# Cached keys in half pages with buffers of their own, cached values in three pages, in a decoder step with two interleaved streams

## The chip, the cores and the metric

The kernel runs on one core of one Trainium2 chip. The metric is device time in microseconds (us) of one execution; the figure for a kernel is the median of its runs. A change of about 0.2% (some 3.6 us) is what a measurement of this kernel can tell from none.

The engines named below: PE multiplies matrices (PEld is its weight load), DVE does elementwise work and reductions, ACT does activations and copies with a scale, POOL does small work and issues gathers, SP issues most plain loads and stores. Each engine takes its instructions in the order in which they stand in its own list, and an instruction that waits holds up all that stand behind it.

## The reference, cut to what matters

One step of a decoder layer for two groups of rows that share the weights: a prompt of 1024 tokens, and 8 sample rows that each attend to 8192 cached tokens. The caches are paged (128 tokens to a page, 64 pages for a sample row, found through a page table).

```python
def fox_sample(q, k, v, logf, k_pool, v_pool, logf_pool, page_table):
    k_all = jnp.concatenate([k_pool[page_table].reshape(B, past, H, hd), ...], axis=1)
    v_all = jnp.concatenate([v_pool[page_table].reshape(B, past, H, hd), ...], axis=1)
    lf_all = jnp.concatenate([logf_pool[page_table].reshape(B, past, H), logf], axis=1)
    c = jnp.cumsum(lf_all, axis=1)
    return fox_attend(q, k_all, v_all, c[:, past:], c, qpos, kpos)     # softmax(q k / 8 + c_q - c_k) v
...
for each group:                                   # prompt, then sample
    x = x + merge_heads(attention, gating, ..., w_o)
    x = x + cross_attend(rmsnorm(x), memory, w_cq, w_co)
    x = x + (silu(gate) * val) @ w_down           # gate, val: causal convolution of rmsnorm(x) @ w_up
y = rmsnorm(x)
```

All numbers are 32-bit floats. The prompt's large products are done as three products of a high and a low part.

## The kernel before, in words

**Two streams.** `prompt()` is a Python generator that writes out the prompt's work stage by stage; `sample()` is another, for the 8 sample rows. The loop at the end of `build` (lines 1923 to 1942) draws from the prompt and, at a rate set by `PACE` for each stage, steps the sample in between. So the text order of the program is an interleaving of both. A scheduler then goes through it with its own model of how long things take, gives out tile buffers as they come free in that model, and fixes the list of each engine. These lists are what the chip runs.

**The sample's first part, `decode()`** (from line 1374). For each sample row `b` there are 16 chunks `ch`; a chunk is 128 x 2048 numbers (1 MB): partition p holds four tokens of half a page. For the keys, `kstep` (line 1425) takes a `KV()` tile, POOL issues an indirect DMA that gathers a chunk (line 1428), DVE multiplies it by the query (lines 1435 and 1444) and sums over each head's 64 elements (1436 and 1448). In stages whose name starts with `att` this is done in four pieces of 512 columns, in some others (`mid`, or while `held`) in two of 1024, otherwise in one of 2048. After 16 chunks there are the softmax steps (`soft_max`, `soft_all`, `soft_exp`). For the values, `vstep` (line 1487) gathers a chunk into a `KV()` tile (1489), and PE multiplies it by the probabilities with four matmuls, one for each quarter of its columns, each on a strip of 32 rows of the accumulator `dv` (1495). Two chunks of values are handled together, 18 chunks after the keys of the same numbers. The gates' cache is gathered by `gates_scan` at chunk 11: an indirect DMA into one `D2()` tile, an ACT copy that swaps tokens and heads (line 1407) into another, and a running sum on DVE (1408).

**The sample's second part, `sample_rest()`** (from line 1611): output projection, cross-attention over 256 memory rows for each sample row, and the gated MLP. Its weights come by POOL's queue in tiles of 1 MB (`page`, line 1568), all in `KV()` tiles. The up-projection works in 11 groups (lines 1761 to 1797): each loads two `KV()` tiles and then issues 64 matmul instructions on `dv` (1774) that alternate between the two tiles, the second one first. ACT copies the result (1786), PE transposes it (1790), ACT copies it back (1791). After the gate (1802 to 1807) the down-projection uses 11 more tiles one after the other (331), and a norm gives the output (1827, 1828).

**Buffers.** `KV()` is one ring of `NKV = 4` tiles of 128 x 2048; `D2()` is a ring of 5 tiles of 128 x 512 that holds queries, gates and many small things of the second part. A tile can be filled again when the last instruction that reads it is done.

**The end of the prompt.** `final` (line 1354) scales the last four tiles of rows by their norm on DVE (1361) and SP stores them (1362). The prompt's large matmuls in its last stage are on lines 272 to 274.

Of the kernel before, what the change touches and what calls it, by code (L numbers as in the profile page):

```python
# [7 lines left out]
F32 = mybir.dt.float32  # L8
# [3 lines left out]
AF = mybir.ActivationFunctionType  # L12
# [37 lines left out]

NKV = 4
VLAG = 2
# [26 lines left out]
def build(nc, tc, ctx, a, phases=None):  # L79
# [42 lines left out]

    def KV():
        return dpool.tile([P, 2048], F32, tag="kv", bufs=NKV, name=nm("kv"))

    def sm(shape, tag, bufs=2, dt=F32):
# [31 lines left out]
    def D2(n=512, dt=F32):  # L158
        return dpool.tile([P, 512], dt, tag="d2", bufs=5, name=nm("d2"))[:, :n]

# [1213 lines left out]
    def decode():  # L1374
# [26 lines left out]

        def gates_scan(b):
            lg = D2()
            nc.gpsimd.indirect_dma_start(lg, None, a["cache_logf"], off(lidx[:, b : b + 1]))
            A = D2()
            Ah = A.rearrange("p (h k) -> p h k", k=64)
            nc.scalar.activation(Ah, lg.rearrange("p (k h) -> p h k", h=8), AF.Copy)
            nc.vector.tensor_tensor_scan(A, rmask, A, 0.0, op0=ALU.mult, op1=ALU.add)
            return A

# [14 lines left out]
        def kstep(b, ch, st):  # L1425
            qb, s = st
            kv = KV()
            nc.gpsimd.indirect_dma_start(kv, None, a["cache_k"], off(kidx[:, b, ch : ch + 1]))  # L1428
            kvv = kv.rearrange("p (k c) -> p k c", c=512)
            if phase[0][:3] == "att":  # L1430

                for i in range(4):
                    yield 0.2
                    with behind(ENG.DVE):
                        nc.vector.tensor_tensor(kvv[:, i, :], kvv[:, i, :], qb, op=ALU.mult)
                        nc.vector.tensor_reduce(
                            s[:, ch * 4 + i, :], kvv[:, i, :].rearrange("p (h d) -> p h d", d=64), axis=AX.X, op=ALU.add
                        )
                return 0.2
            sp = KS if phase[0][:3] == "mid" or held[0] else 1  # L1440
            m = 4 // sp
            with behind(ENG.DVE):
                for i in range(0, 4, m):
                    nc.vector.tensor_tensor(  # L1444
                        kvv[:, i : i + m, :], kvv[:, i : i + m, :], qb.unsqueeze(1).broadcast_to((P, m, 512)), op=ALU.mult
                    )
                for i in range(0, 4, m):
                    nc.vector.tensor_reduce(  # L1448
                        s[:, ch * 4 + i : ch * 4 + i + m, :].rearrange("p k h -> p (k h)"),
                        kvv[:, i : i + m, :].rearrange("p k (h d) -> p (k h) d", d=64),  # L1450
                        axis=AX.X,
                        op=ALU.add,
                    )
            return 1

# [31 lines left out]
        def vstep(b, ch, st, dv, kv):  # L1487
            s = st[1]
            nc.gpsimd.indirect_dma_start(kv, None, a["cache_v"], off(kidx[:, b, ch : ch + 1]))  # L1489
            kvv = kv.rearrange("p (k c) -> p k c", c=512)  # L1490

            def mm(after=None):
                with tc.issue_after(after) if after else behind(ENG.PE):
                    for j in range(4):
                        mmul(  # L1495
                            dv[32 * j : 32 * j + 32, :],
                            s[:, ch * 4 : ch * 4 + 4, :].rearrange("p k h -> p (k h)"),
                            kvv[:, j, :],
                            start=(ch == 1),
                            stop=(ch == 15),  # L1500
                            tile_position=(0, 32 * j),
                        )

            return mm
# [22 lines left out]
        for g in range(8 * 16 + 16 + VLAG + 2):  # L1527
# [8 lines left out]
            if b < 8:  # L1536
                left = yield from kstep(b, ch, st[b])
                if ch == 11:
                    A[b] = gates_scan(b)
                if ch == 13:  # L1540
# [406 lines left out]
_IN = [  # L1947
    "x", "xT", "xs", "xsT", "cache_k", "cache_v", "cache_logf", "cmk", "cmv", "stT", "pt", "mem", "memT",
    "cpack", "gpack", "b_f", "g_sgu_v", "ws00", "bs00", "wsT", "w_in", "w_o", "w_cq", "w_ck", "w_cv", "w_co",
# [8 lines left out]
def layout(np, i):  # L1958
# [15 lines left out]
    for m in range(2):  # L1974
# [13 lines left out]
        "x": f(x), "xT": f(x.T), "xs": f(xs), "xsT": f(xs.T.reshape(8, P, 8).transpose(1, 0, 2)),  # L1988
        "cache_k": f(n["cache_k"]).reshape(-1, 4 * AW), "cache_v": f(n["cache_v"]).reshape(-1, 4 * AW),
        "cache_logf": f(n["cache_logf"]).reshape(-1, 64 * NH),  # L1990
        "cmk": f(n["cache_mem_k"][0]).reshape(NB, NMEM, D), "cmv": f(n["cache_mem_v"][0]).reshape(NB, NMEM, D),
# [43 lines left out]
```

## Time and profile before

| what | value |
|---|---|
| runs, median (lowest to highest) | 1792.71 us (1792.19 to 1794.31) |
| the profiled execution, time | 1793.69 us |
| its span | 1791.7 us |
| PE busy | 1735.9 us, 97% of the span |
| DVE busy | 1399.9 us, 78% |
| ACT busy | 733.5 us, 41% |
| POOL busy | 488.3 us, 27% |
| moved by DMA | 521.06 MB, 291 GB/s on average |
| granted TensorE clock, mean | 0.993 |

How to read it: the shares are averages over stages that differ. The profile of a stretch says which engine was busy throughout; the lists of waits say what ended an engine's idle time; and the timeline of one engine gives the moments at which a buffer came free and the load into it was issued. Line numbers in the profile are those of the kernel before.

### The profile page before, as it was taken

The numbers are of one execution on the slowest core, as the hardware profiler recorded it, in microseconds if no ns is written. First come the engines' busy times: TensorE is split into PE (matmuls) and PEld (weight loads), VectorE is DVE, ScalarE is ACT, GpSimd is POOL, SyncE is SP. The second block draws the span as 40 slices with busy tenths as digits, with TensorE's granted clock in tenths as the row PEclk, the third lists the DMA queues.
The fourth block names the chain that finished last, engine by engine and source line by source line (L and its number), as shares of the span: only waits on it lengthen the run. The fifth ranks groups of instructions, "written<-read, shape, count | busy, mean of one in ns | idle before, by whom it ended". The sixth has DMA issues, their size and how long they took to land.

```text
span 1791.7 us, 25124 instructions
## 1 busy us (share of the span) xinstructions
PE 1735.9 (97%) x9653; PEld 1285.7 (72%) x9653; DVE 1399.9 (78%) x1733; ACT 733.5 (41%) x1374; POOL 488.3 (27%) x461
## 2 busy tenths in 40 slices
PE   8999999889999999999999999999999999999997
PEld 5787777655677666767777777766666778768875
DVE  4689658989788986989999999898885549855344
ACT  6332355566643635333333244335353233333232
POOL 1252234443222332333322223433322112102110
PEclk9999999999999999999999999999999999999999
DMA  8786798777697975779788788988879587568982
GB/s 291 297 304 226 294 334 319 259 264 244 254 403 279 363 299 224 282 285 345 290 301 313 291 317 311 376 306 346 320 280 350 214 306 249 191 260 297 359 310 80
DMA packets 157074, 521.06 MB, mean 291 GB/s; under 512 B 20874, under 2 KB 40842, under 8 KB 124186
## 3 DMA queue, kind: packets, MB, share of 16 engines
q0 software_dynamic: 57168, 341.14, 50.0%
q1 hardware_dynamic: 92874, 165.73, 26.5%
q10 hardware_dynamic: 6912, 12.59, 1.9%
q8 instruction: 76, 1.25, 0.3%
q14 instruction: 44, 0.36, 0.1%
HBM read 495.47 MB, written 23.93 MB: 290 GB/s over the span
## 4 chain that ended last, share of the span: by engine, by line
PE 53%; issue 9%; DMA 8%; DVE 6%; ACT 2%; POOL 2%; POOLq 0%; DVEq 0%; ACTq 0%; SPq 0%
DMA kv<-cache_v,io 6%; PE ba L272 6%; PE ba L274 6%; PE ba L273 6%; PE dv L1495 4%; PE bb L272 3%; PE bb L273 3%; PE bb L274 3%; PE ba L1063 1%; DVE s L1448 1%; PE ba L1064 1%; PE ba L1065 1%; PE dv L331 1%; DMA kv<-cache_k,io 1%; PE dv L1774 1%
## 5 line engine op out<-in xcount | busy, mean ns | idle before, releaser
L235 ACT ACTIVATE wh<-wr 128x1024 fp32r<-128x1024 f32 (+2 forms) x220 | 228.6, 1044 | 443.3 <-PE ba L273 142.3
L236 DVE TENSOR_TENSOR wl<-wr,wh 128x1024 fp32r<-128x1024 f32 (+2 forms) x220 | 262.7, 1200 | 165.1 <-PE ba L274 57.4
L1428 POOL DMA_INDIRECT kv<-cache_k,io x128 | 186.9, 1460 | 606.8 <-DVE s L1448 327.2
L1444 DVE TENSOR_TENSOR kv<-kv,d 128x1024 f32<-128x1024 f32 (+1 forms) x156 | 258.0, 1681 | 32.6 <-DMA kv<-cache_k,io 32.6
L1448 DVE TENSOR_REDUCE s<-kv 128x16 f32<-128x1024 f32 (+1 forms) x156 | 258.4, 1672 | 0.0
L1489 POOL DMA_INDIRECT kv<-cache_v,io x128 | 160.8, 1256 | 239.4 <-PE dv L1495 155.2
L272 PE MATMUL ba<-u,wh 128*128 128x512 f32 x528 | 209.3, 397 | 0.0
L274 PE MATMUL ba<-u,wl 128*128 128x512 f32 x528 | 209.0, 396 | 0.0
L273 PE MATMUL ba<-u,wh 128*128 128x512 f32 x528 | 208.5, 395 | 0.5 <-DVE u L239 0.5
L272 PE MATMUL ba<-wh,u 128*128 128x512 f32 (+1 forms) x495 | 186.1, 379 | 0.9 <-ACT u L235 0.9
L273 PE MATMUL ba<-wl,u 128*128 128x512 f32 (+1 forms) x495 | 185.1, 375 | 1.3 <-DVE wl L236 1.3
L274 PE MATMUL ba<-wh,u 128*128 128x512 f32 (+1 forms) x495 | 183.4, 375 | 0.0
L1495 PE MATMUL dv<-kv,s 128*32 128x512 f32 x1024 | 127.1, 598 | 1.6 <-DMA kv<-cache_v,io 1.6
L274 PEld LDWEIGHTS ba<-u,wl 128*128 128x128 f32 x528 | 99.2, 188 | 29.0 <-issue 6.5
L272 PEld LDWEIGHTS ba<-u,wh 128*128 128x128 f32 x528 | 99.3, 188 | 26.4 <-issue 4.8
L273 PEld LDWEIGHTS ba<-u,wh 128*128 128x128 f32 x528 | 99.2, 188 | 25.2 <-issue 2.3
L272 PEld LDWEIGHTS ba<-wh,u 128*128 128x128 f32 x495 | 93.0, 188 | 25.0 <-issue 6.5
L272 PE MATMUL bb<-u,wh 128*128 128x512 f32 x272 | 108.7, 400 | 0.0
L274 PE MATMUL bb<-u,wl 128*128 128x512 f32 x272 | 108.0, 398 | 0.0
L273 PE MATMUL bb<-u,wh 128*128 128x512 f32 x272 | 107.9, 397 | 0.0
L273 PEld LDWEIGHTS ba<-wl,u 128*128 128x128 f32 x495 | 93.0, 188 | 20.1 <-DVE wl L236 1.9
L274 PEld LDWEIGHTS ba<-wh,u 128*128 128x128 f32 x495 | 92.9, 188 | 19.5 <-issue 1.6
(454 smaller groups left out, 3310.6 us busy)
## 6 DMA issues: line engine op xcount, KB each, us to landing
wr<-w_up SPq DMA_DIRECT2D x88, 512.0 KB
kv<-w_up POOLq DMA_DIRECT2D x22, 1024.0 KB
wr<-w_down SPq DMA_DIRECT2D x40, 512.0 KB
kv<-w_down POOLq DMA_DIRECT2D x11, 1024.0 KB
wr<-w_in SPq DMA_DIRECT2D x16, 512.0 KB
wr<-w_o SPq DMA_DIRECT2D x16, 512.0 KB
wr<-w_cq SPq DMA_DIRECT2D x16, 512.0 KB
wr<-w_co SPq DMA_DIRECT2D x16, 512.0 KB
```

Source lines behind the costliest of these rows:

```text
L235: nc.scalar.activation(h, src, AF.Copy)
L236: nc.vector.tensor_tensor(l, src, h.bitcast(F32), op=ALU.subtract)
L272: mmul(out, sh, mh, start=(i == 0), stop=False)
L273: mmul(out, sh, ml, start=False, stop=False)
L274: mmul(out, sl, mh, start=False, stop=(i == n - 1))
L331: mmul(ps[32 * j : 32 * j + 32, :w], xT[:, k, :] if nk == 8 else xT[:, k * 8 : k * 8 + 32], raw[:, q, j * w : (j + 1) * w], start=(k == 0) ...
L1063: mmul(pss[i], mh[k][:, tb], wh, start=(k == korder[0]), stop=False)
L1428: nc.gpsimd.indirect_dma_start(kv, None, a["cache_k"], off(kidx[:, b, ch : ch + 1]))
L1444: nc.vector.tensor_tensor(kvv[:, i : i + m, :], kvv[:, i : i + m, :], qb.unsqueeze(1).broadcast_to((P, m, 512)), op=ALU.mult)
L1448: nc.vector.tensor_reduce(s[:, ch * 4 + i : ch * 4 + i + m, :].rearrange("p k h -> p (k h)"), kvv[:, i : i + m, :].rearrange("p k (h d) -> ...
L1489: nc.gpsimd.indirect_dma_start(kv, None, a["cache_v"], off(kidx[:, b, ch : ch + 1]))
L1495: mmul(dv[32 * j : 32 * j + 32, :], s[:, ch * 4 : ch * 4 + 4, :].rearrange("p k h -> p (k h)"), kvv[:, j, :], start=(ch == 1), stop=(ch == ...
```

## The change

Keys get a ring of their own, three tiles `kk` of 128 x 1024 (half a chunk, 512 KB), and are gathered in halves from two tensors, `cache_k` and `cache_k1`, which the host lays out as the first and the second half of each chunk; the same index tile serves both. Values, and all of `sample_rest()`, use the `kv` ring, which now has three tiles. `D2()` has three tiles in place of five. Together these take the same room as before: 3 x 4 KB + 3 x 8 KB + 3 x 2 KB against 4 x 8 KB + 5 x 2 KB on each partition. The gates' cache is laid out heads first by the host, so its gather goes straight into the tile of the running sum and the ACT copy is gone; the gather is written at chunk 8, the sum stays at chunk 11. The two chunks of a pair of values are no longer swapped in every other pair.

```diff
-NKV = 4
+NKK = 3
+NKV = 3
...
+    def KK():
+        return dpool.tile([P, 1024], F32, tag="kk", bufs=NKK, name=nm("kk"))
+
+    def VV():
         return dpool.tile([P, 2048], F32, tag="kv", bufs=NKV, name=nm("kv"))
+
+    KV = VV
...
-        return dpool.tile([P, 512], dt, tag="d2", bufs=5, name=nm("d2"))[:, :n]
+        return dpool.tile([P, 512], dt, tag="d2", bufs=3, name=nm("d2"))[:, :n]
...
-        def gates_scan(b):
-            lg = D2()
-            nc.gpsimd.indirect_dma_start(lg, None, a["cache_logf"], off(lidx[:, b : b + 1]))
+        def gates_load(b):
             A = D2()
-            Ah = A.rearrange("p (h k) -> p h k", k=64)
-            nc.scalar.activation(Ah, lg.rearrange("p (k h) -> p h k", h=8), AF.Copy)
+            nc.gpsimd.indirect_dma_start(A, None, a["cache_logf"], off(lidx[:, b : b + 1]))
+            return A
+
+        def gates_scan(A):
             nc.vector.tensor_tensor_scan(A, rmask, A, 0.0, op0=ALU.mult, op1=ALU.add)
...
         def kstep(b, ch, st):
-            kv = KV()
-            nc.gpsimd.indirect_dma_start(kv, None, a["cache_k"], off(kidx[:, b, ch : ch + 1]))
+            att = phase[0][:3] == "att"
+            for h in range(2):
+                kv = KK()
+                src = a["cache_k1" if h else "cache_k"]
+                nc.gpsimd.indirect_dma_start(kv, None, src, off(kidx[:, b, ch : ch + 1]))
+                kvv = kv.rearrange("p (k c) -> p k c", c=512)
+                k0 = ch * 4 + h * 2
...
+                with behind(ENG.DVE):
+                    nc.vector.tensor_tensor(kvv, kvv, qb.unsqueeze(1).broadcast_to((P, 2, 512)), op=ALU.mult)
                     nc.vector.tensor_reduce(
+                        s[:, k0 : k0 + 2, :].rearrange("p k h -> p (k h)"),
+                        kvv.rearrange("p k (h d) -> p (k h) d", d=64),
...
-                            stop=(ch == 15),
+                            stop=(ch == 14),
...
-                two = [(vch - 1, KV()), (vch, KV())]
-                if vch % 4 == 3:
-                    two.reverse()
+                two = [(vch - 1, VV()), (vch, VV())]
```

The scheduler's lists change over the whole program. Three places matter below.

PE's list at the end of the prompt. `ba` and `bb` with `wh`, `wl` are the prompt's last down-projection; `dv` is the sample's accumulator, `kv` its weights. Before, the rows around the last matmul of the sample:

```order
L274 MATMUL bb_14600<-wh_14570,u_14320 128x512
L331 MATMUL dv_14259<-kv_14598,d_2566_14255 32x256 x6
L272 MATMUL ba_14579<-wh_14576,u_14557 128x512
L273 MATMUL ba_14579<-wl_14575,u_14557 128x512
L272 MATMUL bb_14600<-wh_14576,u_14557 128x512
L274 MATMUL ba_14579<-wh_14576,u_14558 128x512
L273 MATMUL bb_14600<-wl_14575,u_14557 128x512
L274 MATMUL bb_14600<-wh_14576,u_14558 128x512
L331 MATMUL dv_14259<-kv_14598,d_2566_14255 32x256 x2
L272 MATMUL ba_14649<-wh_14564,u_14053 128x512
```

In the change, the rows around the last matmul of the prompt (its lines 278 to 280 are lines 272 to 274 before, 1776 is 1774, 1792 is 1790):

```order
L278 MATMUL bb_15138<-wh_15072,u_14695 128x512
L279 MATMUL bb_15138<-wl_15071,u_14695 128x512
L280 MATMUL bb_15138<-wh_15072,u_14696 128x512
L278 MATMUL bb_15138<-wh_15078,u_14933 128x512
L279 MATMUL bb_15138<-wl_15077,u_14933 128x512
L280 MATMUL bb_15138<-wh_15078,u_14934 128x512
L1792 MATMUL ms_13978<-cp,d_2601_13971 128x128
L1776 MATMUL dv_13973<-kv_13976,xg_11916 32x128 x2
L1776 MATMUL dv_13973<-kv_13974,xg_11916 32x128 x2
```

Before, 96 of the prompt's 7119 matmuls stand behind the sample's last one (counted are all instructions outside `decode()`, `sample_rest()` and their helpers). In the change all 7119 stand ahead of the fourth of the 11 groups of the up-projection: 8 groups and the whole down-projection come after them, and the third group stands 10 of the prompt's matmuls ahead of the last. The first group stood behind 6627 of them and now stands behind 7031; the first three groups were 20 and 25 matmuls apart and are now 39 and 39.

POOL's list at the last keys. `kv<-cache_k` or `kk<-cache_k` are gathers of keys, `kv<-cache_v` of values. Before:

```order
L1428 DMA kv_10697<-cache_k,io 128x2048
L1428 DMA kv_10735<-cache_k,io 128x2048
L1489 DMA kv_10748<-cache_v,io 128x2048
L1489 DMA kv_10747<-cache_v,io 128x2048
L1428 DMA kv_10787<-cache_k,io 128x2048
L1428 DMA kv_10825<-cache_k,io 128x2048
```

In the change (its line 1491 is line 1489 before; both halves of the keys are named `cache_k` here):

```order
L1436 DMA kk_11069<-cache_k,io 128x1024
L1436 DMA kk_11105<-cache_k,io 128x1024
L1491 DMA kv_11361<-cache_v,io 128x2048
L1436 DMA kk_11109<-cache_k,io 128x1024
L1491 DMA kv_11579<-cache_v,io 128x2048
L1436 DMA kk_11159<-cache_k,io 128x1024
L1436 DMA kk_11163<-cache_k,io 128x1024
L1491 DMA kv_11580<-cache_v,io 128x2048
```

Two gathers of values in a row have become single ones with keys between. The last softmax of the keys (its result is first used on line 1616) stood behind 5523 matmuls of the prompt and now stands behind 5789; the last values (line 1617 comes next) stood behind 5792 and now behind 6083.

DVE's list at the end, in the change (1021 is 1015 before, the prompt's last sums; 1658 is 1656 and 1829 is 1827, the sample's; 1026 is 1020 and 1367 is 1361, the prompt's last norm and scaling):

```order
L1021 TENSOR_TENSOR u_9855<-bb_15138,u_9855 128x512
L1804 TENSOR_TENSOR d_2685_14628<-d_2564_13713,gp 128x352
L1805 TENSOR_TENSOR d_2685_14628<-d_2685_14628,d_2557_13669 128x352
L1807 MEMSET d_2686_14631 128x24
L1809 TENSOR_TENSOR d_2686_14631<-d_2686_14631,d_2685_14628 128x176
L1658 TENSOR_TENSOR dec_11926<-dv_14635,dec_11926 8x256 x2
L1658 TENSOR_TENSOR vsum_11927<-dv_14635,vsum_11927 8x256 x2
L1578 TENSOR_TENSOR sss_15012<-ss_2741_15007 8x1
L228 TENSOR_SCALAR r1r_15014<-sss_15012 8x1
L1829 SCALAR_TENSOR_TENSOR dec_11926<-dec_11926,r1r_15014,d_2746_15017 8x512
L1829 SCALAR_TENSOR_TENSOR vsum_11927<-vsum_11927,r1r_15014,d_2747_15021 8x512
L1026 TENSOR_TENSOR rq_2770_15160<-sqx_11560 128x1
```

Before, the sample's rows on 1827 stood ahead of the prompt's last five sums on line 1015 and its scalings; now they stand behind all the sums, and the prompt's norms and scalings (from the last row shown) come after them. On SP's list too the stores of the prompt's result (1362) stand behind those of the sample's (1828), before and now.

More of the change, by code (lines that the diff above doesn't have):

```diff
@@ L1426, in kstep @@
             qb, s = st
-            kv = KV()
[L1428 to L1447, printed above, removed]
+            att = phase[0][:3] == "att"
[5 more added lines that the diff above has]
+                k0 = ch * 4 + h * 2
+                if att:
+                    for i in range(2):
+                        yield 0.2
+                        with behind(ENG.DVE):
+                            nc.vector.tensor_tensor(kvv[:, i, :], kvv[:, i, :], qb, op=ALU.mult)
+                            nc.vector.tensor_reduce(
+                                s[:, k0 + i, :], kvv[:, i, :].rearrange("p (h d) -> p h d", d=64), axis=AX.X, op=ALU.add
+                            )
+                    continue
+                with behind(ENG.DVE):
+                    nc.vector.tensor_tensor(kvv, kvv, qb.unsqueeze(1).broadcast_to((P, 2, 512)), op=ALU.mult)
@@ L1453, in kstep @@
                     )
-            return 1
+            return 0.2 if att else 1
         def soft_max(b, st, dt_):
```

16 lines of the change are left out of this document (8 added, 8 removed).

## The prediction

> **What bounds the kernel now.** I read the page's busy shares first, then the stretches, then the chain of waits and POOL's timeline for the sample's second part.
>
> ```profile
> span 1791.7 us, 25124 instructions
> PE 1735.9 (97%) x9653; PEld 1285.7 (72%) x9653; DVE 1399.9 (78%) x1733; ACT 733.5 (41%) x1374; POOL 488.3 (27%) x461
> 800.00:900.00 100.00, 100.00 (x478) 73.11 (x477) 97.00 (x89) 31.89 (x51) 31.80 (x24) 1.00 0.85 323
> 1631.99:1713.00 81.01, 81.01 (x961) 65.16 (x962) 30.67 (x42) 22.82 (x48) 15.66 (x22) 1.00 0.92 346
> 1776.00:1782.00 6.00, 6.00 (x27) 4.86 (x26) 4.84 (x11) 1.74 (x6) 1.64 (x3) 1.00 0.26 108
> 1782.00:1791.70 9.70, 0.40 (x2) 0.00 (x0) 3.36 (x6) 0.72 (x2) 0.54 (x1) 0.66 0.37 150
> ```
>
> In a stretch's row stand its length, the busy time of PE, PEld, DVE, ACT and POOL, the granted clock, the DMA share and GB/s. PE is idle for 1791.7 - 1735.9 = 55.8 us, 9.3 of them after the prompt's last matmul, which ends at 1782.4. So PE's list is the bound, and the sample costs little beyond its own matmuls, because its loads lie under the prompt's. That holds as long as both streams end together. They do, by little:
>
> ```profile
> 1708.13 1.88 PE dv L1774 x64
> 1750.60 1.86 PE dv L331 x32
> 1758.22 0.99 PE dv L331 x12
> 1760.76 0.56 PE dv L331 x4
> 1778.69 0.24 PE ba L274
> ```
>
> This is the chain (start, us). The last up-projection group runs at 1708, the down-projection ends at 1761.3, and only 21 us of the prompt's matmuls follow.
>
> **The change, part by part.**
>
> *Keys in halves.* DVE by form:
>
> ```profile
> L1444 DVE TENSOR_TENSOR kv<-kv,d 128x2048 f32<-128x2048 f32 x68 | 154.4, 2280 | 12.5 <-DMA kv<-cache_k,io 12.5
> L1448 DVE TENSOR_REDUCE s<-kv 128x32 f32<-128x2048 f32 x68 | 154.1, 2273 | 0.0
> L1448 DVE TENSOR_REDUCE s<-kv 128x16 f32<-128x1024 f32 x88 | 104.3, 1208 | 0.0
> L1444 DVE TENSOR_TENSOR kv<-kv,d 128x1024 f32<-128x1024 f32 x88 | 103.5, 1218 | 20.2 <-DMA kv<-cache_k,io 20.1
> L1407 ACT ACTIVATE d<-d 128x512 f32<-128x512 f32 x8 | 9.5, 1192 | 18.5 <-DMA d<-cache_logf,lidx 18.1 <-ACT t L514 0.4
> L1428 POOL DMA_INDIRECT kv<-cache_k,io x128 | 186.9, 1460 | 606.8 <-DVE s L1448 327.2 <-PE dv L1495 127.5 <-DVE s L1436 51.5
> ```
>
> 68 chunks go from 2.280 + 2.273 = 4.553 us to 2 x (1.218 + 1.208) = 4.852: DVE gains 68 x 0.30 = 20 us of work. ACT loses 9.5 us of copies, of which I count nothing, since ACT is 41% busy. POOL issues 128 more gathers, some 128 x 1.46 = 187 us; POOL would be 38% busy, off the path, but its list has gathers of values between those of keys, and a gather that waits for PE to free a `kv` tile holds up the keys behind it, for which DVE waits. Where the stretch from 800 to 900 has DVE at 97%, 20 us cannot all hide. Its bounds for the prompt's stream are 0 (the order already puts the keys later) and 20; I take 5, nearer the lower, since the prompt's weight splits keep their places ahead of the keys.
>
> *The order.* The sample's stages stand later among the prompt's matmuls, as the lists show: the last softmax by 5789 - 5523 = 266, the up-projection's first group by 7031 - 6627 = 404, or 404 x 0.23 = 93 us. The causes visible there are that keys look 1.5 chunks ahead, that a pair of values or of weight tiles now has three tiles to share, and that the small ring has three. Order on an engine is fixed, so a load that lands early cannot bring its matmul forward.
>
> *PE work that moves behind the prompt.* Eight groups, 8 x 1.88 = 15.0, and the down-projection, 5 x 1.86 + 0.99 + 0.56 = 10.9; each of the 13 interruptions also costs the prompt some 0.2 more (a row below, 0.43 for the first matmul after a group, 0.23 otherwise), 2.6. The prompt's last matmul moves from 1782.4 to 1753.9, with the 5 above to 1759. The third group ends ten matmuls, 2.3 us, earlier: 1756.6.
>
> *Eight groups with nothing above them.* A group uses two tiles, so with three only the first load of the next pair runs ahead; the second, which the list multiplies first, needs the tile that the group frees.
>
> ```profile
> 1638.80 1.88 PE dv L1774 x64
> 1640.69 0.43 PE ba L274
> 1641.36 0.23 PE ba L273
> 1640.98 1.43 POOL L1568 DMA_DIRECT2D kv<-w_up  x2 [5.39 <-PE dv L1774]
> 1646.79 1.88 PE dv L1774 x64
> 1744.29 0.71 POOL L1568 DMA_DIRECT2D kv<-w_down  x1 [6.03 <-PE dv L331]
> 1744.00:1745.00 1.00, 1.00 (x17) 0.50 (x10) 0.42 (x1) 0.55 (x2) 0.71 (x1) 1.00 0.98 389
> 1745.00:1746.00 1.00, 1.00 (x5) 0.80 (x5) 0.96 (x2) 0.00 (x0) 0.00 (x1) 1.00 0.93 127
> 1746.00:1747.00 1.00, 1.00 (x6) 0.81 (x5) 0.18 (x2) 0.63 (x1) 0.00 (x0) 1.00 0.45 152
> 1748.00:1749.00 1.00, 1.00 (x6) 0.82 (x5) 0.00 (x0) 0.00 (x0) 0.00 (x0) 1.00 0.98 401
> 1749.00:1750.00 1.00, 1.00 (x6) 0.77 (x6) 0.00 (x0) 0.00 (x0) 0.00 (x0) 1.00 0.10 37
> ```
>
> Before, POOL issues the pair after next 0.3 us after a group, and groups follow each other in some 7 us under a DMA that is 92% busy. The load of 1744.29 is the last of its kind and nearly alone: its last bytes move at 1749.1, 4.8 us after the issue began; the matmul of its predecessors at 1750.60 says nothing closer. I take 5.2 for load and signal, between 4.8 and 6.3. So a period is 0.3 + 5.2 + the group.
>
> The group itself depends on the clock. PE would be busy a quarter of the time, and here is what the clock does when PE pauses:
>
> ```profile
> 370.00:380.00 10.00, 8.41 (x47) 6.08 (x43) 4.31 (x10) 5.36 (x15) 0.00 (x0) 0.73 0.81 295
> L836 PE MATMUL bb<-cp,t x56: 272/276/476, 269.4 to 375.3; 128*128 128x128 f32 x56
> ```
>
> With 1.6 us of pauses in ten the mean clock fell to 0.73, and one form of matmul went from a median of 276 to 476 ns, 1.72 times. I take 1.88 x 1.72 = 3.2 for a group: period 8.7, eight of them 69.6, to 1826.2.
>
> The Trainium skill ("TensorE: Matmul & The Clock Gate", section "HAM oscillation — how this bites in real kernels") describes just this: matmuls of some 2 us, a wait of 3 to 5 us for the next weights, and half the clock each time. The trace has the fall, though in smaller pauses. By its factor of two a group would be 3.76 and the eight 4 us longer in all.
>
> *Down-projection.* Copy, transposes, gate:
>
> ```profile
> 1715.89 0.20 ACT L1791 ACTIVATE d<-ms 128x32 f32<-128x32 f32 x1
> 1718.95 0.34 DVE L1807 TENSOR_TENSOR d<-d,d 128x176 f32<-128x176 f32 x1 [0.56 <-ACT d L1806]
> 1747.00:1748.00 1.00, 1.00 (x6) 0.82 (x5) 0.00 (x0) 0.00 (x0) 0.00 (x0) 1.00 1.02 418
> ```
>
> 3.4 us from the last ACT copy to the gate's end, with the copy and transpose ahead some 5. Tile 0 is there by then; it takes 0.93 x 1.72 = 1.6, so tile 3 is issued at 5 + 1.6 + 0.3 = 6.9 and there at 12.1. The others follow at the DMA's rate, 1 MB at 418 GB/s or 2.6 us with its gaps: seven more, 18.2, and one matmul, 1.6: 32, to 1858.2.
>
> *The end.* DVE takes the prompt's scalings after the sample's.
>
> ```profile
> 1766.29 0.73 DVE L1827 SCALAR_TENSOR_TENSOR vsum<-vsum,r1r,d 8x512 f32<-8x512 f32 x1
> 1776.32 0.16 DVE L1020 TENSOR_TENSOR rq<-sqx 128x1 f32<-128x1 f32 x1 [0.85 <-ACT junk L230]
> 1777.33 1.28 DVE L1361 SCALAR_TENSOR_TENSOR u<-u,rn0r,u 128x1024 f32<-128x1024 f32 x1
> 1785.49 0.75 DVE u L1361
> ```
>
> From 1761.3 to 1767.0 the sample's norm takes 5.7. Then 1.0 to the first scaling, 3 x 1.28 + 2 x 0.75 = 5.3, and 5.5 from the last (1786.2) to the end of the span: 11.8. Sum 1858.2 + 5.7 + 11.8 = 1875.7. The profiled execution took 1793.69 for its span of 1791.7 (2.0 outside) and lies 1.0 above the median: **1877 us**, 84 more than before.
>
> **Rivals.**
>
> *Full clock in the tail* (chance 0.17). For it: the mean before is 0.993, and the load's pause may fall short of what lowers the clock. Against: the slice above. Eight groups at 1.88 save 10.6, the down-projection about 1: 1865.
>
> *The prompt is held up too* (0.14). DVE's 20 us land where it is full, and late keys block its list ahead of the weight splits. For it: 97% in the slice at 800. Against: DVE idles 22% of the span. Price 15 more: 1892, at worst 1907.
>
> *The tail runs at the DMA's rate* (0.05): 2 MB at 418 GB/s is 5.1 us a group if both loads could run ahead. Three tiles speak against it. Saves 8 x 3.6 = 29 and some 4 below: 1844.
>
> *Not slower* (0.03). The split of the rings takes waits out of the decoding stages that lie inside PE's modelled busy time: keys no longer share tiles with values, and POOL waited 127.5 us for PE before a gather of keys. It decides from 84 us saved there. Against: the idle time that PE shows between its first and last matmul is under 50 us, and its matmuls of values,
>
> ```profile
> 1395.04 1.85 PE dv L1495 x16
> L1495 PE MATMUL dv<-kv,s 128*32 128x512 f32 x1024 | 127.1, 598 | 1.6 <-DMA kv<-cache_v,io 1.6
> ```
>
> hold 127.1 us, against 64 pairs at 1.85, 118.4: under 9 us are hidden in them. It would give 1785 or so.
>
> **How the numbers follow.** The forecast has 0.61, with its own range of 1866 to 1889 from the load's bounds (4.8 to 6.3 in eight periods, -3 and +9) and the clock's. Eight times in ten the time should lie between 1848 and 1908: this takes in the first two rivals and leaves out the last two. About 0.2% (3.6 us) is what a measurement can tell. Slower 0.97, within it 0.01, faster 0.02.
>
> **What would show it.** Right: the prompt's last line 274 matmul near 1759, then groups some 8.7 us apart, PE idle between them with POOL's load as the releaser, a clock near half, and stores of the prompt's result last. The first step is wrong if that matmul ends past 1775 (second rival) or before 1740 (last); the period is wrong if groups are 5 or 11 us apart; the clock if groups keep 1.88. The prediction as a whole is wrong if no more than a group or two is left when the prompt ends.

## The result and the profile after

| | before | after |
|---|---|---|
| median of 5 runs (lowest to highest), us | 1792.19 (1790.94 to 1794.31) | 1926.67 (1914.38 to 1932.33) |
| profiled execution and its span, us | 1793.69, 1791.7 | 1926.67, 1924.9 |
| PE idle in the span, us | 55.8 | 147.2 |

The ratio is 1.0746, with a 95% interval of 1.0704 to 1.0789: the change costs 134 us. The forecast was 1877 with a range to 1908, so the sign was right and the time lies outside. The span is 133.2 us longer. PE's busy time grew by 41.8 us for the same 9653 matmuls, which ran at a lower clock (0.958 on average against 0.993), and PE's idle time by 91.4. Rows of the page of the changed kernel; the last one is from its fourth part, the chain of work that ended last:

```profile
span 1924.9 us, 25436 instructions
PE 1777.7 (92%) x9653; PEld 1308.5 (68%) x9653; DVE 1410.9 (73%) x1869; ACT 727.6 (38%) x1369; POOL 622.3 (32%) x589
PEclk9999998899999998999999999999999999999865
DMA kk<-cache_k,io 8%; PE ba L279 7%; PE ba L280 7%; PE ba L278 7%; PE dv L1497 5%; PE bb L278 4%; PE bb L280 3%; PE bb L279 3%; DMA kv<-w_up 3%; DVE s L1450 2%; DVE kk L1449 2%; DVE wl L242 2%; POOL kk L1436 2%; DMA kv<-w_down 1%; DMA kv<-x 1%
```

Gathers of keys make up 8% of that chain; in the kernel before they made up 1% of it.

The granted clock falls in the seventh, eighth and sixteenth of the 40 slices, and in the last three. The next two fences cut both traces into stages that hold about the same matmuls (the counts of PE stand in the first brackets). Columns: stretch, its length, busy time of PE, PEld, DVE, ACT, POOL, then clock, DMA share and GB/s. Before:

```profile
0.00:160.00 160.00, 149.92 (x849) 121.46 (x850) 111.99 (x126) 67.71 (x101) 42.08 (x31) 1.00 0.78 278
160.00:712.00 552.00, 526.41 (x2923) 383.08 (x2922) 454.50 (x642) 276.07 (x583) 180.94 (x187) 0.98 0.81 296
712.00:1218.00 506.00, 501.75 (x2413) 372.70 (x2412) 471.27 (x460) 181.49 (x289) 154.36 (x111) 1.00 0.83 310
1218.00:1782.40 564.40, 557.85 (x3474) 408.43 (x3472) 359.13 (x502) 207.53 (x402) 110.40 (x132) 1.00 0.74 274
```

After, with the tail as a fifth stage and, in the last two rows, the middle of it and its down-projection:

```profile
0.00:160.00 160.00, 148.99 (x833) 120.93 (x834) 102.34 (x146) 63.44 (x96) 47.49 (x43) 0.98 0.76 259
160.00:760.00 600.00, 545.66 (x2944) 392.84 (x2943) 472.00 (x675) 277.27 (x586) 236.95 (x240) 0.96 0.79 279
760.00:1265.00 505.00, 503.42 (x2424) 375.02 (x2423) 460.13 (x527) 179.29 (x290) 205.99 (x157) 1.00 0.84 309
1265.00:1801.00 536.00, 527.95 (x2761) 386.59 (x2759) 364.91 (x497) 197.50 (x365) 111.08 (x120) 1.00 0.66 236
1801.00:1924.90 123.90, 51.63 (x698) 33.10 (x696) 11.52 (x26) 10.13 (x34) 20.81 (x29) 0.59 0.64 239
1840.00:1872.00 32.00, 15.26 (x255) 13.24 (x259) 0.00 (x0) 1.43 (x6) 4.27 (x6) 0.55 0.62 231
1875.40:1908.70 33.30, 20.12 (x176) 6.52 (x176) 0.00 (x0) 0.00 (x0) 5.74 (x9) 0.55 0.86 320
```

Two things are to be seen. **The second stage takes 600 us in place of 552**: 28.7 us more of PE idle (54.3 against 25.6), and 19.3 more of busy PE. That these are not more matmuls is seen when both traces are cut ahead of one and the same matmul of the prompt, which starts at 711.96 before and at 758.8 after:

```profile
0.00:711.95 711.95, 676.27 (x3769) 504.51 (x3770) 566.49 (x767) 343.73 (x683) 223.02 (x218) 0.99 0.80 292
0.00:758.77 758.77, 693.42 (x3769) 512.76 (x3770) 573.72 (x819) 339.48 (x680) 284.44 (x283) 0.96 0.79 275
```

The same 3769 matmuls end 47 us later: 30 us of idle PE, and 17 in matmuls that take longer at the lower clock. The third stage, where DVE is fullest, loses nothing. **The tail** is 124 us long, where before 9.3 us lay behind the prompt's last matmul. The fourth stage is 28 us shorter, since it holds 713 matmuls less; the tail has 698. So the prompt ends 48 - 1 - 28.4 = 18.6 us later, at 1801 and not at 1782.4.

The tail in order of time (start, us, engine, line; in brackets the idle time before and its releaser), two of its eight groups:

```profile
1804.35 3.34 PE L1776 MATMUL dv<-kv,xg 128*32 128x128 f32 x64 [3.11 <-DMA kv<-w_up]
1807.99 1.42 POOL L1570 DMA_DIRECT2D kv<-w_up  x2 [7.65 <-PE dv L1776]
...
1813.41 3.64 PE L1776 MATMUL dv<-kv,xg 128*32 128x128 f32 x64 [4.91 <-DMA kv<-w_up]
1817.34 1.42 POOL L1570 DMA_DIRECT2D kv<-w_up  x2 [7.93 <-PE dv L1776]
...
1822.62 3.64 PE L1776 MATMUL dv<-kv,xg 128*32 128x128 f32 x64 [4.77 <-DMA kv<-w_up]
1872.71 0.71 POOL L1570 DMA_DIRECT2D kv<-w_down  x1 [7.89 <-PE dv L1776]
...
1906.74 1.93 PE L337 MATMUL dv<-kv,d 128*32 128x256 f32 x16 [0.66 <-DMA kv<-w_down]
```

A group ends, POOL loads into the tile that it freed, and the next group starts 5.4 (1807.99 to 1813.41) or 5.3 us (1817.34 to 1822.62) later, takes 3.64, and so on. This is the bare tail of the forecast. From the same rows the terms of the sum can be set beside what came (the third group's end is taken 0.3 us ahead of POOL's issue at 1798.91):

| term, us | forecast | measured | miss |
|---|---|---|---|
| end of the third group, near the prompt's last matmul | 1756.6 | 1798.6 | +42.0 |
| eight groups, to 1872.4 | 69.6 | 73.8 | +4.2 |
| down-projection, to 1908.7 | 32.0 | 36.3 | +4.3 |
| norm, scalings, stores, to the end | 17.5 | 16.2 | -1.3 |
| span | 1875.7 | 1924.9 | +49.2 |

So the tail was forecast within some 7 us of 126, and the prompt's stream was missed by 42. Where that stream loses time is read from DVE's waits. The first row is the wait of DVE's multiplication for a gather of keys, the second that of POOL's gather of values for PE to free a tile (total us, times, longest). Before:

```profile
DVE kv L1444 <- DMA kv<-cache_k,io: 32.6, 18, 5.6
POOL kv L1489 <- PE dv L1495: 155.2, 41, 11.4
```

After:

```profile
DVE kk L1449 <- DMA kk<-cache_k,io: 74.3, 47, 5.5
POOL kv L1491 <- PE dv L1497: 254.1, 50, 40.1
```

And here is one such wait in DVE's list of the changed kernel, with POOL's and PE's rows around it (`wl` on line 242 is the low part of a weight of the prompt):

```profile
219.99 0.94 POOL L1436 DMA_INDIRECT kk<-cache_k,io  x1 [0.30 <-issue]
226.15 1.21 DVE L242 TENSOR_TENSOR wl<-wr,wh 128x1024 fp32r<-128x1024 f32 x1
228.94 1.23 DVE L1449 TENSOR_TENSOR kk<-kk,d 128x1024 f32<-128x1024 f32 x1 [1.59 <-DMA kk<-cache_k,io]
230.09 1.22 DVE L242 TENSOR_TENSOR wl<-wr,wh 128x1024 fp32r<-128x1024 f32 x1
231.36 0.50 PE L279 MATMUL ba<-wl,u 128*128 128x512 f32 x1 [0.29 <-DVE wl L242]
```

The half page issued at 219.99 reaches DVE at 228.94. DVE stands still for 1.59 us. Behind the waiting multiplication in its list is a weight split, and PE reaches the matmul that needs this split at once when it is done, after an idle time that DVE ends. Each single stall is small, and the splits are only a small part of them: of the second stage's 54.3 us of idle PE, splits end 2.3. DVE's results in all end 23.9 (before 7.2), ACT's 28.1 (17.3), in many short waits, most of them in the prompt's attention; what ACT itself had waited for was not followed back. By my reading of the trace (start of the same matmul of the prompt after, less that before) the prompt lies 13 us behind at 235 us, 30 at 360, 41 at 600, 47 at 760, and no more after that.

The theory for the experiments: **keys look too short a way ahead**. With four whole tiles, DVE frees one and three are left, 3 x 4.55 = 13.7 us of its key work; with three half tiles two are left, 2 x 2.43 = 4.9 us. A gather of keys takes 7.2 us to land (median, issues of the changed kernel). So keys come late, and DVE's list passes the delay to whatever work of the prompt stands behind them. Rivals: the halves themselves (POOL's 128 more gathers, DVE's longer work); values, which now wait 254 us in POOL's list ahead of keys; the small parts (gates, ring `d2`, order of two values); and for the tail, that only the third tile is missing.

### The profile page after: what moved, and what is told of

Same layout as the page of the kernel before. It is cut to its first block, busy times and chain, and to the rows that moved or that the text cites. A ratio compares the mean times of both kernels' runs of the same rounds, so it can differ in the third digit from the quotient of the medians.

```text
span 1924.9 us, 25436 instructions
## 1 busy us (share of the span) xinstructions
PE 1777.7 (92%) x9653; PEld 1308.5 (68%) x9653; DVE 1410.9 (73%) x1869; ACT 727.6 (38%) x1369; POOL 622.3 (32%) x589
## 4 chain that ended last, share of the span: by engine, by line
PE 51%; DMA 18%; DVE 12%; issue 12%; POOL 3%; ACT 2%; SPq 0%; POOLq 0%; DVEq 0%; ACTq 0%
DMA kk<-cache_k,io 8%; PE ba L279 7%; PE ba L280 7%; PE ba L278 7%; PE dv L1497 5%; PE bb L278 4%; PE bb L280 3%; PE bb L279 3%; DMA kv<-w_up 3%; DVE s L1450 2%; DVE kk L1449 2%; DVE wl L242 2%; POOL kk L1436 2%; DMA kv<-w_down 1%; DMA kv<-x 1%
## 5 line engine op out<-in xcount | busy, mean ns | idle before, releaser
L1436 POOL DMA_INDIRECT kk<-cache_k,io x256 | 333.3, 1302 | 551.0 <-DVE s L1450 399.6
L242 DVE TENSOR_TENSOR wl<-wr,wh 128x1024 fp32r<-128x1024 f32 (+2 forms) x220 | 263.1, 1200 | 95.7 <-PE ba L280 24.1
L1449 DVE TENSOR_TENSOR kk<-kk,d 128x1024 f32<-128x1024 f32 x224 | 271.6, 1218 | 74.9 <-DMA kk<-cache_k,io 74.3
L1450 DVE TENSOR_REDUCE s<-kk 128x16 f32<-128x1024 f32 x224 | 269.1, 1210 | 0.9
L1491 POOL DMA_INDIRECT kv<-cache_v,io x128 | 147.7, 1154 | 310.0 <-PE dv L1497 254.1
L278 PE MATMUL ba<-wh,u 128*128 128x512 f32 (+1 forms) x495 | 188.7, 383 | 3.7 <-DVE u L794 2.2
L280 PE MATMUL ba<-wh,u 128*128 128x512 f32 (+1 forms) x495 | 184.9, 378 | 0.0
L1497 PE MATMUL dv<-kv,s 128*32 128x512 f32 x1024 | 132.2, 616 | 7.1 <-DMA kv<-cache_v,io 4.3
L278 PEld LDWEIGHTS ba<-wh,u 128*128 128x128 f32 x495 | 94.7, 191 | 28.5 <-issue 8.4
```

The costliest lines, as they stand in the source:

```text
L242: nc.vector.tensor_tensor(l, src, h.bitcast(F32), op=ALU.subtract)
L278: mmul(out, sh, mh, start=(i == 0), stop=False)
L280: mmul(out, sl, mh, start=False, stop=(i == n - 1))
L1436: nc.gpsimd.indirect_dma_start(kv, None, src, off(kidx[:, b, ch : ch + 1]))
L1449: nc.vector.tensor_tensor(kvv, kvv, qb.unsqueeze(1).broadcast_to((P, 2, 512)), op=ALU.mult)
L1450: nc.vector.tensor_reduce(s[:, k0 : k0 + 2, :].rearrange("p k h -> p (k h)"), kvv.rearrange("p k (h d) -> p (k h) d", d=64), axis=AX.X, op ...
```

## The experiments

Times of each kernel are medians beside runs of the kernel before on the same chip, which lay at 1790.7 to 1794.4.

**The shared ring cut to three, nothing else (before, edited).**

```
-NKV = 4
+NKV = 3
```

> The kernel before with three shared tiles (NKV = 3) and nothing else: keys in whole chunks by one gather, five small tiles. Its lists put the first up-projection group behind 6946 of the 7055 large matmuls that the two kernels share (after: 6967, before: 6563). Theory (fewer tiles ahead: the order leaves the second part for the end, and DVE waits for late keys): a bare tail of seven or eight groups 9 us apart as in the change, last prompt matmul between 1765 and 1800, 1870 to 1915 in all. Rival (the doubled gathers and the halves make the difference): the prompt ends near 1760 as the prediction had it, and the whole near 1870 at most; a second rival (the tail belongs to the separate rings): no tail, 1795.

Measured: 1963.05 us (1950.56 to 1972.66), ratio 1.0957 [1.0913, 1.1001]. It is slower than the change itself, and both the time and the prompt's end lie beyond what was expected of the theory (1915 and 1800 at most).

```profile
DVE kv L1444 <- DMA kv<-cache_k,io: 124.5, 44, 9.2
POOL kv L1489 <- DVE s L1448: 265.8, 43, 9.7
```

DVE's wait for keys is 124.5 us with whole pages and single gathers, and the prompt's last matmul ends at 1843. So the lag needs no halves; too few tiles are enough. The second row shows what a shared ring adds: gathers of values wait for tiles that keys hold (39.1 us before).

**Halves without their own ring (before, edited):** two tensors, two gathers a chunk into the two halves of one shared tile, DVE in halves.

```
-            nc.gpsimd.indirect_dma_start(kv, None, a["cache_k"], off(kidx[:, b, ch : ch + 1]))
+            for h in range(2):
+                kh = kv[:, h * 1024 : h * 1024 + 1024]
+                src = a["cache_k1" if h else "cache_k"]
+                nc.gpsimd.indirect_dma_start(kh, None, src, off(kidx[:, b, ch : ch + 1]))
```

> The kernel before with keys gathered in halves from two tensors into the two halves of one shared tile: 128 more gathers on POOL and 20 us more on DVE, four shared tiles as before. Theory (look-ahead, not the halves): within 8 us of before, 1790 to 1800. Rival (the halves themselves stall the prompt by 40 us): 1825 to 1840, with POOL or DVE named where PE waits.

Measured: 1805.31 us, ratio 1.0089 [1.0066, 1.0112], some 16 us. DVE's wait for keys is 30.0 us (22 times), as before; the prompt's last matmul ends at 1792.2, 9.8 later than before. That is 5 us over what was expected of the theory and 20 under what the rival asked for: the halves cost something, but a small part of 134.

**Gates, ring `d2` of three and no swapped pair alone (before, edited).**

```
-        return dpool.tile([P, 512], dt, tag="d2", bufs=5, name=nm("d2"))[:, :n]
+        return dpool.tile([P, 512], dt, tag="d2", bufs=3, name=nm("d2"))[:, :n]
...
-                if vch % 4 == 3:
-                    two.reverse()
```

with the gates' part of the change as it stands there.

> The kernel before with the three small parts alone: gates heads first and gathered at chunk 8, three small tiles in place of five, pairs of values not swapped. All theories: no more than 4 us from before (9.5 us of ACT copies go, ACT is 41% busy). Rival (three small tiles hold up the queries and the second part): 1800 or more.

Measured: 1794.64 us, ratio 1.0017 [1.0004, 1.003]. Some 3 us lie here, 5.4 at the interval's upper end.

**Two half-page buffers in place of three (the change, edited).** Ring `d2` goes back to five in this kernel and the next.

```
-NKK = 3
+NKK = 2
```

> The change with two half tiles for keys in place of three and five small tiles: look-ahead of keys cut by a third, everything else as in the change. Theory (late keys block DVE's list): DVE waits for keys rise from 74 us to 120 or more, the prompt's last large matmul, at 1801 in the change although less of the sample lies ahead of it, does not come earlier than 1801. Rivals (values' three tiles, or the number of gathers): DVE's wait for keys stays near 74 and the prompt ends some 15 us earlier, at 1785, since all eleven groups now stand behind it.

Measured: 2029.02 us, ratio 1.1332 [1.1301, 1.1362].

```profile
DVE kk L1449 <- DMA kk<-cache_k,io: 161.0, 95, 7.3
```

Half the look-ahead more than doubles the wait, and the prompt's last matmul ends at 1840.0 although all eleven groups stand behind it. The ring for values is the one of the change, so the number of half-page tiles does this by itself; ring `d2`, the other difference, was worth 5.4 us at most in the kernel above.

**Four half-page buffers, two pages for values (the change, edited).**

```
-NKK = 3
-NKV = 3
+NKK = 4
+NKV = 2
```

> The change with four half tiles for keys, two tiles for values and the second part, five small tiles: two chunks of keys ahead as in the kernel before, but no tile ahead for a pair of values. Theory (late keys are what holds up the prompt): DVE's wait for keys falls from 74 us to 45 or less, the prompt's last large matmul comes at 1785 or earlier (1801 in the change); the tail is longer, groups 10 to 12 us apart, some 1935 in all. Rival (values that wait for their tiles hold up POOL's list): DVE's wait stays or rises, the prompt ends at 1800 or later.

Measured: 1935.93 us, ratio 1.0787 [1.0744, 1.0831]. The waits, then the end of the prompt and POOL's issues behind it:

```profile
POOL kv L1491 <- PE dv L1497: 296.4, 56, 15.6
DVE kk L1449 <- DMA kk<-cache_k,io: 21.1, 21, 3.7
```

```profile
1767.15 0.40 PE L280 MATMUL bb<-wh,u 128*128 128x512 f32 x1
...
1781.58 1.43 POOL L1570 DMA_DIRECT2D kv<-w_up  x2 [10.42 <-PE dv L1776]
1793.11 1.43 POOL L1570 DMA_DIRECT2D kv<-w_up  x2 [10.10 <-PE dv L1776]
1804.90 1.43 POOL L1570 DMA_DIRECT2D kv<-w_up  x2 [10.36 <-PE dv L1776]
```

This is the run that tells most. Two causes come apart: with one half-page tile more, DVE hardly waits and the prompt ends at 1767.5, 33 us earlier than in the change. With one whole tile less, no load runs ahead in the tail and its pairs of loads are 11.5 to 11.8 us apart, so that the gain is lost again. Values wait even longer in POOL's list than in the change (296 against 254 us) while keys are on time, which speaks against the values as the cause; the kernel changes both rings, so by itself it doesn't shut them out.

Four half-page tiles beside three whole ones would have separated this fully. They take 4 KB more on each partition than the rings of the change, and no run took these from another ring.

**The tail's release made finer (the change, edited):** an up-projection group multiplies with its first tile to the end, and then with its second.

```
-            for k in range(8):
-                for j in (2, 3, 0, 1):
+            for r in range(2):
+                for k in range(8):
+                    for j in (2 * r, 2 * r + 1):
...
-                            rvs[j // 2][:, k, j % 2, :],
+                                rvs[r][:, k, j % 2, :],
```

> The change with the 64 matmuls of an up-projection group in another order: the tile that is loaded first is used up first, then the other. A tile comes free in the middle of a group, so three tiles are enough to load ahead. Theory (a group waits for the one load that had no tile): groups 5.5 to 7 us apart in the bare tail, though the matmuls of a group take longer, 1890 to 1908 in all. Rival (the rate of the loads or the clock sets the period): 9 us as in the change, 1925 or more.

Measured: 1902.39 us, ratio 1.0612 [1.0584, 1.0639], 24 us better than the change. POOL's issues between 1806 and 1840, and the stretch:

```profile
1809.22 0.71 POOL L1570 DMA_DIRECT2D kv<-w_up  x1 [5.18 <-PE dv L1777]
...
1833.66 0.71 POOL L1570 DMA_DIRECT2D kv<-w_up  x1 [1.92 <-PE dv L1777]
```

```profile
1806.00:1840.00 34.00, 24.93 (x359) 21.72 (x358) 0.69 (x1) 2.57 (x11) 7.13 (x10) 0.90 0.89 326
```

There are nine issues of one tile, so eight periods, in 24.4 us: 3.06 us a tile, 6.1 a group in place of 9.2. The clock is back at 0.90, and the DMA's share rises from 0.62 to 0.89. So the period of the tail was indeed set by a tile that came free too late. The shorter period is only part of the gain, though. The lists changed too: groups under the prompt stand 8.2 us apart in place of 11.2 and take 3.3 us each in place of 2.0, the prompt ends at 1806.9, and six groups are left behind it, not eight. In the two profiled executions, 32.8 us apart, the groups behind the prompt take 36.3 us (71.3 in the change), the down-projection 3.6 less, and the prompt ends 5.8 later.

**Two gathers a chunk alone (before, edited),** and **DVE's halves alone (before, edited):**

```
-            nc.gpsimd.indirect_dma_start(kv, None, a["cache_k"], off(kidx[:, b, ch : ch + 1]))
+            for h in range(2):
+                src = a["cache_k1" if h else "cache_k"]
+                nc.gpsimd.indirect_dma_start(kv[:, h * 1024 : h * 1024 + 1024], None, src, off(kidx[:, b, ch : ch + 1]))
```

```
-            sp = KS if phase[0][:3] == "mid" or held[0] else 1
+            sp = 2
```

> The kernel before with each chunk of keys gathered by two DMAs from two tensors into the halves of one shared tile, DVE's work as before. The halves alone cost 0.9% (16 us). If POOL's 128 more gathers make that: 10 us or more here, 1801 to 1808. If DVE's 20 us make it: within 4 us of before.

> The kernel before with one gather to a chunk, but DVE multiplies and sums keys in halves of 1024 columns in all stages outside the attention stages: 20 us more work on DVE, both products ahead of both sums. If DVE's extra work makes the 16 us of the halves: 1800 to 1808. If POOL's gathers do: within 4 us of before.

Measured: 1802.95 us, ratio 1.0055 [1.0036, 1.0073], and 1797.7 us, 1.0026 [1.0011, 1.0041]. Together 0.81%, near the 0.89% of both: of the halves' cost two thirds are the gathers, and DVE's 20 us of work cost some 5 (2 to 7 by the interval), as the forecast had taken.

**The gates' part alone (before, edited).**

```
-            Ah = A.rearrange("p (h k) -> p h k", k=64)
-            nc.scalar.activation(Ah, lg.rearrange("p (k h) -> p h k", h=8), AF.Copy)
...
+                if ch == 8:
+                    A[b] = gates_load(b)
```

> The kernel before with the gates' cache heads first and its gather at chunk 8, nothing else. Eight ACT copies of 1.2 us and eight small tiles go. All theories: within 3 us of before, 1789 to 1794; if three small tiles made the 0.17% of the small parts, no loss at all here.

**The gates' part with `d2` of three, and the room that this frees given to two other rings (before, edited):** `NT` 7 to 9 in one kernel, `NU` 18 to 19 in the other.

> The gates heads first, three small tiles in place of five, and the 4 KB that this frees given to the prompt: nine tiles t2 in place of seven. If waits for these tiles are among the 47 us that PE idles between its first and last matmul: 3 to 8 us faster than before. If the weight splits and the stage boundaries make that idle time: within 3 us of before.

> The gates heads first, three small tiles in place of five, and the 4 KB that this frees given to the prompt's large tiles: 19 in place of 18. If loads that wait for these tiles are among PE's idle time: 3 to 8 us faster than before. Otherwise as the small parts alone, 1793 to 1799.

Measured: 1797.77 us, 1.0021 [1.0006, 1.0035]; 1797.94, 1.0023 [1.0008, 1.0039]; 1797.57, 1.0014 [1.0001, 1.0027]. All three are at the edge of what can be told from no change, and none is faster than before: no gain from the tiles `t2` or the prompt's large tiles is seen. The first lies 4 us over what was expected and shows the loss of the small parts without the three small tiles, so nothing points to these as its cause.

**Three tiles in the second part only (before, edited).** One of the four shared tiles is taken when the second part begins and held to its end (one memset and one small addition more); keys and values keep all four.

```
+        hold = KV()
+        nc.vector.memset(hold[:, 0:1], 0.0)
...
+        nc.vector.tensor_tensor(sm([8, 1], "hold", 1), hold[:8, 0:1], xs[1][:, 0:1], op=ALU.add)
```

> The kernel before, in which the second part of the sample holds one of the four shared tiles from its start to its end (a one-column memset and one small sum are added), so keys and values have four tiles and the second part three. Its lists put the first up-projection group behind 6648 of the 7055 matmuls that the two kernels share (before 6563, the change 6967), the last group 17 matmuls ahead of the prompt's end, the down-projection behind it. Theory (tail and stalls add up from separate causes): prompt's last matmul at 1770 to 1776, then 30 to 34 us of down-projection and 17 of endings, 1812 to 1832 in all, no lag before 1400 us. Rival (the second part's three tiles make most of the change's 134 us): 1880 or more. Rival (they cost nothing, the keys' delay makes the tail): 1795 or less.

Measured: 1821.7 us, ratio 1.0155 [1.0129, 1.0181], 28 us.

```profile
1762.97 1.42 POOL L1568 DMA_DIRECT2D kv<-w_down  x2 [9.81 <-PE dv L1776]
1770.84 0.71 POOL L1568 DMA_DIRECT2D kv<-w_down  x1 [6.45 <-PE dv L331]
...
1791.15 0.71 POOL L1568 DMA_DIRECT2D kv<-w_down  x1 [3.45 <-PE dv L331]
```

DVE waits 30.9 us for keys, as before, and the prompt doesn't lag. Here the eleven groups stay under the prompt, which ends at 1766.8, somewhat earlier than expected, and only the down-projection is bare. So a missing tile costs 28 us in the second part by itself. Where keys and values had three tiles too, in the first experiment, eight groups stood behind the prompt as in the change: with fewer tiles for keys and values the scheduler puts the whole sample later in the list.

The runs that bear on the prompt's lag, side by side. Lag is taken at the matmul that before starts at 711.96 us; up to it, every kernel of the table has run the same matmuls but for a handful of records (3765 to 3769). The third column is the wait for keys of the multiplication outside the attention stages (line 1444, or 1449 in the change) in the whole run, the fourth all of DVE's waits for gathers of keys up to that matmul:

| kernel | key work ahead, us | wait for keys, us | of all waits for keys, up to the matmul | lag, us |
|---|---|---|---|---|
| four halves, own ring | 7.3 | 21.1 | 13.8 | 10 |
| before: four whole tiles, shared | up to 13.7 | 32.6 | 11.9 | 0 |
| halves in four whole tiles, shared | up to 13.7 | 30.0 | 13.3 | -1 |
| the change: three halves, own ring | 4.9 | 74.3 | 53.0 | 47 |
| three whole tiles, shared | up to 9.1 | 124.5 | 54.1 | 51 |
| two halves, own ring | 2.4 | 161.0 | 95.7 | 82 |

Key work ahead is worked out: the tiles left when DVE frees one, by 2.43 us a half and 4.55 us a whole; a shared ring has less of it, by what values hold. Lag follows the wait up to the same point, within some 10 us: 41 us more of waiting than before go with 47 of lag, 42 with 51, 84 with 82. The loads are not what became slower: a gather of keys lands after 7.2 us (median) in the change, 7.1 in the halves that share four tiles, 5.8 with two half tiles, where the wait is longest. The lag of 10 with four halves is not explained by waits, and halves in a shared ring have none at this point; it stays open.

By stretches, the span's 133 us are 18.7 by which the prompt ends later (its lag of 47, less the sample's work that left it), and 114.5 by which what follows it is longer (123.8 against 9.3). By causes they were not fully divided: three tiles in the second part alone are worth 28 us, the halves 16, the small parts 3. The remaining 87 of 134 are a difference and were not measured by themselves: they hold the 33 us by which a fourth half-page tile let the prompt end earlier, and the eight groups that stand behind the prompt. Nor need the parts add up: the shared ring cut to three costs 171 us alone.

## Why the prediction was right or wrong

*What bounds the kernel, and that both streams end together by little:* right. A tail of 124 us took the place of 9.3, and 117 was forecast.

*Keys in halves: wrong, and here is the failed step.* The prediction said: "Its bounds for the prompt's stream are 0 (the order already puts the keys later) and 20; I take 5, nearer the lower, since the prompt's weight splits keep their places ahead of the keys." Those bounds held only DVE's 20 us of longer work, and that work does cost some 5, as DVE's halves alone showed. The term that was left out, put at nothing, is waiting: work of the prompt that stands behind a late key in DVE's list waits with it. DVE's wait for keys rose from 32.6 to 74.3 us, the prompt lay 47 us behind at 760, and the third group and the prompt's end came 42 us later than forecast. The reason given, that weight splits keep their places ahead of the keys, misses most of this: splits end 2.3 of the second stage's 54.3 us of idle PE, other work of DVE 21.6. The text had the pieces. It named the key "for which DVE waits", and it read that keys look 1.5 chunks ahead, but it priced neither against the time that a gather takes to land. It also looked in the wrong stage: at 800 to 900, where DVE is 97% busy, the change loses nothing, and the 47 us are lost before 760, where DVE has idle time. The keys' gathers did cost POOL more, 146 us (333.3 less 186.9) in place of the 187 assumed, as a half's gather takes 1.302 us and not 1.460.

*The second rival, "The prompt is held up too", is what happened,* with its cause (late keys block DVE's list) and its sign (the matmul past 1775); that they block it ahead of the weight splits is the small part again. Its price was too small: 15 us on top of the forecast, against 42. "DVE idles 22% of the span" was no argument against it, since that idle time contains the waits.

*PE work that moves behind the prompt:* right, and near in size: eight groups and the down-projection stood behind it, and the fourth stage is 28.4 us shorter where 28.5 were taken off. The run with four halves, where keys are on time, ends the prompt at 1767.5 with nine groups behind it, 13.6 over the 1753.9 of this step.

*Eight groups with nothing above them:* right, 9.2 us each against 8.7. Load and signal took 5.3 to 5.6 (eight groups), 5.2 was taken. The group took 3.2 to 3.7, most often 3.64, where 3.2 was taken: the clock fell to 0.55, and the factor of 3.64 to 1.88 us is 1.94, not 1.72. The Trainium skill's factor of two for a clock gated by such waits ("TensorE: Matmul & The Clock Gate", section "HAM oscillation — how this bites in real kernels") fits this trace better than the slice that I preferred. The rival of full clock in the tail falls by the same rows.

*Down-projection:* mis-sized by 4.3. Most tiles took 1.94 us where 1.6 was taken, and the eleven tiles ran from 1875.4 to 1908.7, 3.0 a tile, where 2.6 was taken from the DMA's rate.

*The end:* right within 1.3. *The tail at the DMA's rate* did not come by itself; the kernel that frees the tiles one by one came near it, at 6.1 us a group. *Not slower* falls: the 127.5 us that POOL waited for PE ahead of gathers of keys are gone from the list of waits, and POOL now waits 399.6 us for DVE there and 254.1 for PE ahead of values.

## What to carry to other kernels

Before a ring is split or shrunk, work out for each of its users what is left to do when one buffer comes free, and set it against the time that a load takes to land; the page's busy shares don't show this. An engine with an in-order list passes a late load on to everything behind it, so what is blocked can be another stream than the one whose buffers were cut: cut two traces ahead of the same instruction to see in which stage it falls behind. And look for who else uses the ring: here the second part, which has nothing to do with keys, lost 28 us to a missing tile, and in the change, freeing tiles one at a time gave 24 us back.

## What was unexpected of the hardware

Pauses of some 5 us between bursts of PE kept the granted clock at 0.55 in the middle of the tail: a group of 64 matmuls went from 1.88 to 3.64 us. In the down-projection behind it the pauses were only 0.6 to 2.9 us, and the clock stayed at 0.55: a tile took 1.94 us in place of 0.93. In the kernel that frees tile after tile, PE's waits for a tile were 1.2 to 1.6 us and the clock was 0.90. So the length of the pauses alone does not tell the clock here; what else enters was not tested.

Splitting a gather in two at equal bytes costs time even where DVE does not wait longer for it: 0.55% [0.36, 0.73], with DVE's wait for keys at 28.6 us (32.6 before). The Trainium skill ("DMA: Bandwidth & Descriptors", section "Measured (HBM→SBUF, 128 partitions, SWDGE, issued from GpSimd)") advises transfers of 1 MiB and more for the rate; these went from 1 MB to 512 KB, so the sign agrees. The packets of this queue took 51.0% of the 16 DMA engines' time in place of 50.0%, and POOL was busy for 669 us in place of 488. Whether the loss lies in the transfers or in POOL's longer list was not separated.

Taking eight copies of ACT away (9.5 us of work, 18.5 of waiting) gained nothing: 1.0021 [1.0006, 1.0035].
